# Sums of output-weight blocks on VectorE, in place, and a last token tile in new PSUM banks

## The chip, the cores and the metric

The kernel runs on one core of a Trainium2 chip. The metric is device time in microseconds (us) for one execution. A profiled execution of the kernel also leaves a trace: the start and duration of each instruction on each engine, what ended the idle time in front of it, and the clock that TensorE was granted. Engine names are those of the profile: PE is TensorE (PEld its weight loads), DVE is VectorE, ACT is ScalarE, POOL is GpSimd, SP is SyncE, whose queue issues most DMAs.

## What is computed

One hybrid decoder layer on x (1024 tokens x 1024 features, float32). A first norm and a combined input projection feed two branches, a retention and a gated linear recurrence; both are gated, concatenated to 2048 columns, and pass one output projection, a residual add and a final norm. Cut to what matters here:

```python
h = x
xn = rms_norm(h, norm_in_g)
q, k, v, g_ret, x_lru, g_lru = jnp.split(einsum('btd,de->bte', xn, w_in), IN_SPLITS, axis=-1)
y_ret = group_norm_heads(chunkwise_retention(q, k, v)) * silu(g_ret)   # 1024 columns
y_lru = rg_lru(conv(x_lru)) * silu(g_lru)                              # 1024 columns
h = h + einsum('bte,ed->btd', concatenate([y_ret, y_lru]), w_out)      # w_out: 2048 x 1024
return rms_norm(h, norm_out_g)
```

The change lies in the last part: the retention's half of the output projection, y_ret (1024 x 1024) times the upper half of `w_out` (1024 x 1024), and the norm behind it.

## The kernel before

Every product of two float32 matrices is made from three matmuls in a rounded format: each operand is split by `split` into a high part (a cast on ACT, L106) and a low part (a subtraction on DVE, L107), and `mm3` (L112) issues high x high, high x low and low x high. A block of 256 rows x 512 columns of weights is one tile of 128 partitions x 2 x 512, so a cast or subtraction of it is 128x1024 (called wide below); a piece of 128 tokens x 512 columns is 128x512 (half-wide).

The program runs in stages: input projection, gates and recurrence; then `w_out`'s lower half (the recurrence's share) with the retention's work put in between as `fillers`; then the last stage. Instructions are written in Python order, but a scheduler sets the order on each engine's own queue, and each queue is worked in order: what waits at its head holds all behind it.

The last stage computes four quarter products (two token halves x two column halves) with seven products instead of eight. They run in the order P1, P2, P5, P6, P7, P3, P4; each has four token tiles (t = 0 to 3) of 12 matmuls of 128x512. The weight operands, with Wkc the block of row half k and column half c:

- P1: W11, P2: W21, P3: W22
- P5: W11+W12, P6: W11+W12+W22, P7: W12+W22, P4: W11+W12+W22+W21

`w_load` (L893) makes such a sum while it loads: SP loads the first block into a tile pair, and POOL issues one DMA for each further block that adds it to what lies there (L901, `accum_op`). One accumulating DMA must have landed before the next of the same tile is issued. `w_parts` (L905) then splits both tiles into high and low parts. On the other side `combine` (L188, DVE) makes sums of the retention's output blocks `ys`, which `y_block` (L911) reads back from memory, and `y_parts` (L917) splits them.

PSUM has eight banks here. `A[t]` holds P1, then P6, P7 and P4 on top of it; `E[t]` holds P5 and P3; P2 uses the banks that E takes afterwards. `block_add` (L993 to 996) adds a bank to the result tile `h`. After P7, A and E are both added to the second token half; P3 may only write `E[t]` once that is done. P4 closes `A[t]` for t = 0 to 2; its last tile, t = 3, is made in two halves of 256 columns in the same bank `A[3]`, so that the norm of the first half can start. Then follows the norm of each of the eight token tiles (`square`, `norm_first`, `norm_last`, L956 to 986): a square with its row sum on ACT (L958), a square root on ACT (L975), a few 128x1 operations on DVE, a scaling of one column half on ACT (L982) and of the other on DVE (L984), and two stores.

SBUF on the left holds the retention's tiles (`kn`, `sm`, `gch`, `st`, `yn`, `ot`, pool stack `ret`) to the end of the program, with the final norm's `gain2` and `junk` above them.

Of the kernel before, what the change touches and what calls it, by code (L numbers as in the profile page):

```python
# [11 lines left out]
F32R = mybir.dt.float32r  # L12
I32 = mybir.dt.int32
AF = mybir.ActivationFunctionType
ALU = mybir.AluOpType

P = 128
# [23 lines left out]
def hybrid_layer(  # L41
# [17 lines left out]
    pe, act, dve, pool, sp = nc.tensor, nc.scalar, nc.vector, nc.gpsimd, nc.sync  # L59
# [3 lines left out]
    HALF = D // 2  # L63
# [3 lines left out]
    def pool_on(side, name, bufs):  # L67
        return tc.tile_pool(name=name, bufs=bufs, side=side, reuse_waits="tile")
# [6 lines left out]
    def psum():  # L75
        return ps_p.tile([P, 512], F32, name="pp", tag="pp")
# [622 lines left out]
    for j in range(2):  # L699
# [4 lines left out]
    op = {n: ctx.enter_context(pool_on("right", n, k)) for n, k in (  # L704
        ("wraw", 3), ("y0", 2), ("wo", 10), ("qkc", 4), ("yl", 14), ("vc", 4), ("h", 8))}
# [24 lines left out]
    for t in range(NT):  # L730
        r = op["h"].tile([P, T], F32, name="h", tag="h")
# [8 lines left out]
    yl = {}  # L740
# [12 lines left out]
        fill()  # L753
    ph_stack.close()
    ph_next = {}
    ret = ctx.enter_context(ExitStack())
    mask_sb = gwp.tile([P, H, P], F32, name="mask", tag="gw")
    sp.dma_start(out=mask_sb, in_=mask_in)
    for name, n in (("kn", 2), ("sm", 2), ("gch", 3), ("st", 4),
# [1 line left out]
        ph_next[name] = ret.enter_context(pool_on("left", name, n))  # L761

    ph_next["vc"] = op["vc"]
    fin = ctx.enter_context(pool_on("left", "fin", 1))
    junkp = ctx.enter_context(pool_on("left", "junk", 2))


    def heads(f):
# [117 lines left out]
    wt, ys, xop = {}, {}, {}  # L886

    def block(pl):
        return [op[pl].tile([P, 2, 512], F32, name="blk", tag=pl) for _ in range(2)]

    wr = {}

    def w_load(name, pl, *blocks):  # L893

        r = wr[name] = block(pl)
        for i in range(2):
            for j, (kh, ch) in enumerate(blocks):
                src = w_out[kh * HALF + i * 256:kh * HALF + (i + 1) * 256, ch * HALF:(ch + 1) * HALF] \
                    .rearrange("(k p) c -> p k c", p=P)
                if j:  # L900
                    pool.dma_start(out=r[i], in_=src, accum_op=ALU.add)  # L901
                else:
                    sp.dma_start(out=r[i], in_=src)

    def w_parts(name):  # L905
        r = wr.pop(name)
        wt[name] = Parts(op["yl"], "yl")
        for i in range(2):
            wt[name].put(i, r[i])

    def y_block(f, th):  # L911
        ys[f, th] = block("wo" if f or th else "y0")
# [4 lines left out]
    def y_parts(name, src):  # L917
        pl = "qkc" if name in ("P2", "P6", "P3") else "wo" if name == "P4" else "yl"
        xop[name] = Parts(op[pl], pl)
        for i in range(2):  # L920
            xop[name].put(i, src[i])

    for dh in range(2):
        cols = slice(dh * HALF, (dh + 1) * HALF)
        w_cur = w_o
        for t in range(NT):
            if dh == 0 and 0 < t < NT - 1:
                load_yl(t + 1)
            if dh == 0 and t == 2:
                w_o = group(D, HALF, (0,))  # L930
            ps = psum()
            unit_o(ps, yl[t], w_cur, slice(0, HALF), (3, 7) if dh == 0 else (2, 5, 7))
            r = hres[t][:, cols]
            with tc.issue_after(last_load[0].ins):
                sp.dma_start(out=r, in_=x[t * P:(t + 1) * P, cols])
            dve.tensor_tensor(out=r, in0=ps, in1=r, op=ALU.add)
            if dh == 0 and t == NT - 2:
                w_o += group(D, HALF, (2, 4, 6))
            if dh == 1 and t == 2:
                w_load("P1", "wraw", (0, 0))  # L940
                w_parts("P1")
            if dh == 1 and t == 4:
                w_load("P2", "wraw", (1, 0))
                w_parts("P2")
            if dh == 1 and t == 5:
                y_block(0, 0)
                y_parts("P1", ys[0, 0])
            if dh == 1 and t == 6:
                y_block(1, 0)
                w_load("P5", "wraw", (0, 0), (0, 1))  # L950
    gain2 = fin.tile([P, T], F32, name="gain2")
    sp.dma_start(out=gain2, in_=g_out.partition_broadcast(P))
    dve.tensor_tensor(out=gain2, in0=gain2, in1=gain2, op=ALU.add)
# [34 lines left out]
    def product(name, ps, t, first, last, cols=slice(0, 512)):  # L988
        for k in range(4):
            mm3(ps, xop[name].token(k, t), tuple(a[:, cols] for a in wt[name].row(k)),  # L990
                first and k == 0, last and k == 3)

    def block_add(t, th, ch, ps, op_=ALU.add, cols=slice(0, 512)):  # L993
        r = hres[4 * th + t][:, ch * HALF + cols.start:ch * HALF + cols.stop]
        dve.tensor_tensor(out=r, in0=r, in1=ps, op=op_)  # L995
        return r

    A, E = [psum() for _ in range(4)], []
    for t in range(4):
        product("P1", A[t], t, True, False)  # L1000
        block_add(t, 0, 0, A[t])
        fill()
        if t == 0:
            y_parts("P2", ys[1, 0])
    while fillers:
        fill()
    y_block(0, 1)
    y_block(1, 1)
    w_parts("P5")
    combine(s1 := block("wo"), ys[0, 1], ys[1, 1], ALU.subtract)  # L1010
    y_parts("P5", s1)
    for t in range(4):
        ps = psum()
        product("P2", ps, t, True, True)
        block_add(t, 0, 0, ps)
        norm_first(t, 0)
    w_load("P6", "wraw", (0, 0), (0, 1), (1, 1))
    w_parts("P6")
    combine(s1, s1, ys[0, 0], ALU.subtract)
    y_parts("P6", s1)  # L1020
    for t in range(4):
        E.append(psum())
        product("P5", E[t], t, True, False)
    w_load("P7", "wraw", (0, 1), (1, 1))
    w_parts("P7")
    s3 = ys[0, 1]
    combine(s3, ys[0, 0], s3, ALU.subtract)
    y_parts("P7", s3)
    for t in range(4):
        product("P6", A[t], t, False, False)  # L1030
        block_add(t, 0, 1, A[t], ALU.subtract)
    w_load("P4", "y0", (0, 0), (0, 1), (1, 1), (1, 0))
    w_load("P3", "wraw", (1, 1))
    w_parts("P3")
    s4 = ys[1, 0]
    combine(s4, s1, s4, ALU.add)
    y_parts("P3", s4)
    for t in range(4):
# [1 line left out]
        block_add(t, 1, 1, A[t], ALU.subtract)  # L1040
        block_add(t, 1, 1, E[t])
        norm_first(4 + t, 1)
    y_parts("P4", ys[1, 1])
    w_parts("P4")
    for t in range(4):
        product("P3", E[t], t, False, True)
        r = block_add(t, 0, 1, E[t])
        square(ssum[:, t, 1:2], r)
        norm_last(t, 1, ssum[:, t, 1:2])
    for t in range(4):  # L1050
        mean, part = ssum[:, 4 + t, 0:1], ssum[:, 4 + t, 1:2]
        cuts = [0, 512] if t < 3 else [0, 256, 512]
        for c0, c1_ in zip(cuts, cuts[1:]):
            cols = slice(c0, c1_)
            product("P4", A[t][:, cols], t, False, True, cols)
            square(part, block_add(t, 1, 0, A[t][:, cols], ALU.add, cols))
            if c1_ < 512:
                dve.scalar_tensor_tensor(out=mean, in0=part, scalar=1.0 / D, in1=mean,
                                         op0=ALU.mult, op1=ALU.add)
                part = small.tile([P, 1], F32, name="part", tag="part")  # L1060
        norm_last(4 + t, 0, part)
# [69 lines left out]
```

## Time and profile before

| what | value |
|---|---|
| time, median of 3 runs | 774.28 us (772.71 to 774.65) |
| the profiled execution: time / span of its instructions | 770.49 us / 768.7 us |
| PE busy | 729.0 us, 95% of the span |
| DVE busy | 575.8 us, 75% |
| ACT busy | 426.2 us, 55% |
| POOL busy | 17.4 us, 2%, of which 17.2 us are the 14 accumulating DMAs |
| mean granted PE clock | 0.981 |
| chain that ended last, by engine | PE 59%, ACT 14%, DVE 13%, DMA 7% |

The whole-span shares are averages. The stage of the change starts near 663 us, where P1's first matmul runs, and lasts to the end, so it has to be read by itself: in which stretches PE waits, and what ends each wait.

### The profile page before, as it was taken

To read this page: it belongs to the slowest core of one execution; us is meant where nothing else is said; L and a number is where in the kernel's file an instruction comes from. 1 tells how busy PE (TensorE), PEld (TensorE's weight loads), DVE (VectorE), ACT (ScalarE), POOL (GpSimd) and SP (SyncE) were. 2 spreads that over 40 slices of the span, in tenths; PEclk is the share of its full clock that TensorE was granted. 3 is DMA by queue.
4 is the path that set the end of the run, shared out by engine and by line. 5 is a ranking of instruction groups with operands and counts; after the bars stand their busy time and mean duration, and the time that the engine had idled before them with its cause. 6 is when DMAs were issued, how large, how long until landed. Compare 5 with 4: busy or idle time off the path is not lost.

```text
span 768.7 us, 9387 instructions
## 1 busy us (share of the span) xinstructions
PE 729.0 (95%) x3448; PEld 604.5 (79%) x3448; DVE 575.8 (75%) x950; ACT 426.2 (55%) x649; POOL 17.4 (2%) x18
## 2 busy tenths in 40 slices
PE   6989999999999999999999999997999999999764
PEld 5777888887787888788788888887899998888553
DVE  6998647669977968976899887874675667589355
ACT  6785435695599689679533333335453454244134
POOL 0000000000000000000000000000000011111100
PEclk9999999999999999999999999999999999999987
DMA  8752712140214213422445544599987686687534
GB/s 303 277 192 83 246 54 69 55 133 32 76 48 165 69 55 99 134 83 75 145 125 128 132 111 109 146 284 291 311 274 259 212 263 152 191 185 143 82 83 164
DMA packets 98015, 116.07 MB, mean 151 GB/s; under 512 B 5169, under 2 KB 66737, under 8 KB 97969
## 3 DMA queue, kind: packets, MB, share of 16 engines
q1 hardware_dynamic: 94160, 108.13, 44.5%
q0 software_dynamic: 3808, 7.34, 6.1%
q8 instruction: 27, 0.44, 0.2%
q14 instruction: 20, 0.16, 0.1%
HBM read 86.09 MB, written 29.36 MB: 150 GB/s over the span
## 4 chain that ended last, share of the span: by engine, by line
PE 59%; ACT 14%; DVE 13%; DMA 7%; issue 5%; SPq 1%; POOL 0%; ACTq 0%; DVEq 0%; POOLq 0%
PE pp L112 51%; PE pp L796 2%; PE pp L835 2%; PE pp L834 2%; DMA bt<-in_w_in 1%; DVE xc L561 1%; PE pp L817 1%; DVE wq L107 1%; DVE y L614 1%; PE pp L856 1%; DMA xt<-in_x 1%; ACT wq L106 1%; DMA graw<-in_gate_w 1%; DMA vc<-v_d 1%; ACT L601 1%
## 5 line engine op out<-in xcount | busy, mean ns | idle before, releaser
L112 PE MATMUL pp<-wh,wq 128*128 128x512 f32 x960 | 301.6, 391 | 1.8 <-DVE cy L471 0.9
L112 PEld LDWEIGHTS pp<-wh,wq 128*128 128x128 f32 x960 | 179.9, 188 | 42.8 <-ACT cy L461 2.4
L112 PE MATMUL pp<-wl,wq 128*128 128x512 f32 x480 | 186.9, 389 | 0.0
L112 PEld LDWEIGHTS pp<-wl,wq 128*128 128x128 f32 x480 | 90.1, 188 | 18.6
L112 PE MATMUL pp<-wo,yt 128*128 128x512 f32 x384 | 97.9, 402 | 0.0
L112 PEld LDWEIGHTS pp<-wo,yt 128*128 128x128 f32 x384 | 70.4, 191 | 13.0
L107 DVE TENSOR_TENSOR wq<-t,wq 128x1024 fp32r<-128x1024 f32 x40 | 48.7, 1221 | 38.8 <-ACT wq L106 31.7
L106 ACT CAST wq<-t 128x1024 fp32r<-128x1024 f32 x40 | 41.7, 1051 | 31.6 <-PE pp L112 26.6
L112 PE MATMUL pp<-wh 128*128 128x512 f32 x112 | 45.9, 410 | 8.3 <-ACT wh L106 8.3
L112 PE MATMUL pp<-wh,w 128*128 128x512 f32 x160 | 52.9, 391 | 0.1
L112 PE MATMUL pp<-wl,wh 128*128 128x512 f32 x112 | 45.1, 404 | 0.0
L106 ACT CAST ylh<-blk 128x1024 fp32r<-128x1024 f32 x20 | 20.5, 1049 | 43.2 <-DMA blk<-in_w_out 28.8
L112 PE MATMUL pp<-wh,wl 128*128 128x512 f32 x112 | 43.9, 396 | 0.1
L112 PEld LDWEIGHTS pp<-wh,w 128*128 128x128 f32 x160 | 30.0, 188 | 6.8 <-DVE w L107 0.5
L461 ACT COPY cy<-pp 128x512 f32<-128x512 f32 x20 | 11.6, 580 | 41.8 <-PE pp L112 41.2
L848 ACT ACTIVATE yn<-pp,nb,rs_y 128x128 f32<-128x128 f32 x64 | 24.0, 457 | 17.0 <-DVE nb L846 17.0
L901 POOL DMA_DIRECT2D blk<-in_w_out x14 | 17.2, 1228 | 713.8 <-DVE ot L858 622.6
L107 DVE TENSOR_TENSOR yll<-blk,ylh 128x1024 fp32r<-128x1024 f32 x20 | 24.1, 1221 | 11.3 <-ACT ylh L106 11.2
L112 PEld LDWEIGHTS pp<-wh 128*128 128x128 f32 x112 | 21.9, 195 | 13.5 <-ACT wh L106 8.7
L112 PE MATMUL pp<-ylh,qkch 128*128 128x512 f32 x48 | 20.3, 422 | 12.3 <-DVE h L995 12.3
L112 PE MATMUL pp<-wl,w 128*128 128x512 f32 x80 | 31.1, 389 | 0.0
L422 ACT CAST wq<-wraw 128x512 fp32r<-128x512 f32 x40 | 22.9, 617 | 9.3 <-PE pp L112 8.4
(183 smaller groups left out, 1358.5 us busy)
## 6 DMA issues: line engine op xcount, KB each, us to landing
wraw<-in_w_in SPq DMA_DIRECT2D x40, 512.0 KB, 4.9
qkc<-qk_d SPq DMA_DIRECT2D x16, 512.0 KB, 5.9
blk<-in_w_out SPq DMA_DIRECT2D x14, 512.0 KB, 4.5
blk<-in_w_out POOLq DMA_DIRECT2D x14, 512.0 KB, 5.7
bt<-in_w_in SPq DMA_DIRECT2D x20, 256.0 KB, 5.4
xA<-in_xT SPq DMA_DIRECT2D x16, 256.0 KB, 5.4
v_d<-vo SPq DMA_DIRECT2D x16, 256.0 KB, 2.5
xt<-in_x SPq DMA_DIRECT2D x8, 512.0 KB, 4.4
```

Source lines behind the costliest of these rows:

```text
L106: act.copy(out=hi, in_=src)
L107: dve.tensor_tensor(out=lo, in0=src, in1=hi.bitcast(F32), op=ALU.subtract)
L112: pe.matmul(ps, a, b, start=first and j == 0, stop=last and j == 2, skip_group_check=True)
L422: act.copy(out=h[:, j], in_=b)
L461: act.copy(out=self.cy[:, :TH], in_=self.A)
L561: dve.scalar_tensor_tensor(out=xc[:, d:], in0=c[:, :T - d], scalar=cw[3 - d], in1=xc[:, d:], op0=ALU.mult, op1=ALU.add)
L601: act.activation(out=a, in_=r, func=AF.Exp, scale=c1[:, b:b + 1])
L796: heads(lambda h, hs: pe.matmul(psc[:, hs], k[:, hs], q[:, hs], start=True, stop=True))
L834: pe.matmul(po[:, hs], q[:, hs], st[:, h], start=True, stop=False)
L835: pe.matmul(po[:, hs], sm[:, h], vn[:, hs], start=st is None, stop=True)
L848: heads(lambda h, hs: act.activation(out=yn[:, hs], in_=po[:, hs], func=AF.Identity, scale=rs[:, h:h + 1], bias=nb[:, h:h + 1]))
L901: pool.dma_start(out=r[i], in_=src, accum_op=ALU.add)
```

## The change

It does five things. `w_load` loads one plain block, by SP alone; POOL issues no DMA any more. `w_parts` takes a second block and adds it to the first on DVE, in place, before the split: P5's sum is W11 += W12, P6's adds W22 to that, P4's adds W21, and P7's is W12 += W22; that makes eight wide additions. The retention's space is given back before the stage, and a new pool `lw` of six tiles lies there: the blocks W22 and W21 and the low part of P4's weights (its high part goes to `y0`). P4's split is written between P7's token tiles, not after them. And A[3] is added to `h` by itself during P3, after which P4's last tile starts anew in two fresh PSUM banks, one for each half.

```diff
+    fin = ctx.enter_context(pool_on("left", "fin", 1))
+    junkp = ctx.enter_context(pool_on("left", "junk", 2))
+    ret = ExitStack()
...
-    def w_load(name, pl, *blocks):
-
+    def w_load(name, pl, kh, ch):
         r = wr[name] = block(pl)
         for i in range(2):
-            for j, (kh, ch) in enumerate(blocks):
...
-                if j:
-                    pool.dma_start(out=r[i], in_=src, accum_op=ALU.add)
-                else:
-                    sp.dma_start(out=r[i], in_=src)
...
+    def w_parts(name, src, add=None, dst=None):
+
+        w = wt[name] = object.__new__(Parts)
+        w.hi, w.lo = [[op[pl].tile([P, 2, 512], F32R, name="wt", tag=pl) for _ in range(2)]
+                      for pl in (("y0", "lw") if name == "P4" else ("yl", "yl"))]
         for i in range(2):
-            wt[name].put(i, r[i])
+            r = wr[src][i]
+            if add:
+                o = wr[dst or src][i]
+                dve.tensor_tensor(out=o, in0=r, in1=wr[add][i], op=ALU.add)
+                r = o
+            wt[name].put(i, r)
...
+    while fillers:
+        fill()
+    ret.close()
+    op["lw"] = ctx.enter_context(pool_on("left", "lw", 6))
     A, E = [psum() for _ in range(4)], []
+    w_load("12", "wo", 0, 1)
     for t in range(4):
         product("P1", A[t], t, True, False)
         block_add(t, 0, 0, A[t])
-        fill()
...
-    w_parts("P5")
+    w_load("22", "lw", 1, 1)
+    w_load("21", "lw", 1, 0)
+    w_parts("P5", "11", "12")
...
-    w_load("P6", "wraw", (0, 0), (0, 1), (1, 1))
-    w_parts("P6")
+    w_parts("P6", "11", "22")
...
-    w_load("P7", "wraw", (0, 1), (1, 1))
-    w_parts("P7")
+    w_parts("P7", "12", "22")
...
-    w_load("P4", "y0", (0, 0), (0, 1), (1, 1), (1, 0))
-    w_load("P3", "wraw", (1, 1))
-    w_parts("P3")
+    w_parts("P3", "22")
...
         norm_first(4 + t, 1)
-    y_parts("P4", ys[1, 1])
-    w_parts("P4")
+        if t == 1:
+            w_parts("P4", "11", "21")
+        elif t == 2:
+            y_parts("P4", ys[1, 1])
     for t in range(4):
         product("P3", E[t], t, False, True)
+        if t == 3:
+            block_add(t, 1, 0, A[t])
...
-            product("P4", A[t][:, cols], t, False, True, cols)
-            square(part, block_add(t, 1, 0, A[t][:, cols], ALU.add, cols))
+            ps = A[t][:, cols] if t < 3 else psum()[:, cols]
+            product("P4", ps, t, t == 3, True, cols)
+            square(part, block_add(t, 1, 0, ps, ALU.add, cols))
```

Up to the retention's last token tile the order on every engine is the one before. Three places of the last stage are shown. The first is DVE after product P7. In the kernel before, `yll_6026` is the low part of P4's second weight tile and the `h` rows are the additions of A (pp_5596) and E (pp_5809, pp_5822) that P3 has to wait for:

```order
L995 TENSOR_TENSOR h_3798<-h_3798,pp_5809 128x512 [waits DVE_49]
L107 TENSOR_TENSOR yll_6026<-blk_5912,ylh_6024 128x1024 [waits DMASW5_49,Activation_49]
L964 TENSOR_SCALAR ssum_5592<-ssum_5592 128x1 [waits Activation_49]
L965 TENSOR_TENSOR h_3798<-h_3798,gain2_5589 128x512 [waits DVE_49]
L995 TENSOR_TENSOR h_3799<-h_3799,pp_5596 128x512 [waits PE_49]
L995 TENSOR_TENSOR h_3799<-h_3799,pp_5822 128x512 [waits DVE_49]
```

and now, where L909 is the new addition of W21 and `wt_5978`, `wt_5979` are the low parts of P4's weights:

```order
L997 TENSOR_TENSOR h_3796<-h_3796,pp_5600 128x512 [waits PE_49]
L107 TENSOR_TENSOR wt_5978<-blk_5548,wt_5976 128x1024 [waits DVE_49]
L997 TENSOR_TENSOR h_3796<-h_3796,pp_5798 128x512 [waits DVE_49]
L997 TENSOR_TENSOR h_3797<-h_3797,pp_5601 128x512 [waits PE_49]
L909 TENSOR_TENSOR blk_5549<-blk_5549,blk_5681 128x1024 [waits DMAHW2_49]
L966 TENSOR_SCALAR ssum_5590<-ssum_5590 128x1 [waits Activation_49]
L967 TENSOR_TENSOR h_3796<-h_3796,gain2_5587 128x512 [waits DVE_49]
L997 TENSOR_TENSOR h_3797<-h_3797,pp_5811 128x512 [waits DVE_49]
L107 TENSOR_TENSOR wt_5979<-blk_5549,wt_5977 128x1024 [waits Activation_49]
```

P4's low part still stands between these additions, but what it waited for from the accumulating DMAs (DMASW5) is now an addition on DVE itself of a block that SP loads.

The second place is SP's queue around P1. In the kernel before, `blk<-o_d` are the retention's outputs of the second token half and `blk<-in_w_out` the first blocks for P5's second tile, P6 (two), P4, P3 (two), P4:

```order
L859 DMA o_d_77<-ot_5569 128x4x128 [waits DVE_49]
L903 DMA blk_5758<-in_w_out 128x2x512 [waits DMAHW4_49,DMASW0_49,DVE_49]
L914 DMA blk_5661<-o_d_77 128x2x512 [waits DMAHW5_49,DMAHW3_49,DMAHW6_49,DMAHW0_49,PE_49]
L914 DMA blk_5662<-o_d_77 128x2x512 [waits PE_49]
L903 DMA blk_5835<-in_w_out 128x2x512 [waits DMASW1_49,DVE_49]
L903 DMA blk_5836<-in_w_out 128x2x512 [waits DMASW3_49,DVE_49]
L903 DMA blk_5911<-in_w_out 128x2x512 [waits DMAHW1_49,DVE_49]
```

and now, where blk_5604 and blk_5605 are W12, blk_5676 and blk_5677 W22, and blk_5680 and blk_5681 W21:

```order
L896 DMA blk_5604<-in_w_out 128x2x512 [waits DMAHW0_49,PE_49]
L896 DMA blk_5605<-in_w_out 128x2x512 [waits DMAHW1_49,PE_49]
L916 DMA blk_5668<-o_d_77 128x2x512 [waits DMAHW3_49,DMAHW6_49,DMAHW2_49,PE_49]
L916 DMA blk_5669<-o_d_77 128x2x512 [waits PE_49]
L859 DMA o_d_77<-ot_5567 128x4x128 [waits DMAHW4_49,DVE_49]
L896 DMA blk_5676<-in_w_out 128x2x512 [waits DMAHW5_49,Activation_49]
L896 DMA blk_5677<-in_w_out 128x2x512 [waits Activation_49]
L916 DMA blk_5672<-o_d_77 128x2x512 [waits DMAHW7_49,DMAHW4_49,PE_49]
L916 DMA blk_5673<-o_d_77 128x2x512 [waits DMAHW0_49,PE_49]
L896 DMA blk_5680<-in_w_out 128x2x512 [waits DMAHW1_49]
L896 DMA blk_5681<-in_w_out 128x2x512 [waits DMAHW2_49]
```

All weight loads now stand close together, two of them ahead of the retention's blocks, and behind the last of them come only the stores of the result.

The third place is DVE at the start of the stage. `ot` is the gated output of the retention's last token tile, which SP stores and reads back for P5, and blk_5548, blk_5549 are the two tiles of W11. In the changed kernel there stands:

```order
L909 TENSOR_TENSOR blk_5548<-blk_5548,blk_5604 128x1024 [waits DMAHW0_49]
L858 TENSOR_TENSOR ot_5567<-pp_5562,gch_5299 128x512 [waits DMAHW6_49,DMAHW4_49,PE_49]
L938 TENSOR_TENSOR h_3799<-pp_5552,h_3799 128x512 [waits PE_49]
L107 TENSOR_TENSOR wt_5686<-blk_5548,wt_5684 128x1024 [waits Activation_49]
L909 TENSOR_TENSOR blk_5549<-blk_5549,blk_5605 128x1024 [waits DMAHW7_49,DMAHW1_49]
```

where before stood

```order
L858 TENSOR_TENSOR ot_5569<-pp_5564,gch_5299 128x512 [waits DMAHW7_49,DMAHW5_49,PE_49]
L936 TENSOR_TENSOR h_3799<-pp_5554,h_3799 128x512 [waits PE_49]
L107 TENSOR_TENSOR yll_5667<-blk_5548,ylh_5665 128x1024 [waits DMASW0_49,Activation_49]
L995 TENSOR_TENSOR h_3792<-h_3792,pp_5593 128x512 [waits PE_49]
L995 TENSOR_TENSOR h_3793<-h_3793,pp_5594 128x512 [waits PE_49]
```

The first new addition, which waits for the load of W12, stands ahead of the retention's last `ot`.

## Rows read from the trace of the kernel before

**Rows 1.** Busy time by stretch: PE, PEld, DVE, ACT, POOL, PEclk, DMA, GB/s.

```profile
663.70:718.30 54.60, 54.60 (x241) 44.86 (x239) 39.88 (x47) 20.00 (x26) 8.63 (x8) 1.00 0.71 159
718.30:740.30 22.00, 9.78 (x37) 7.66 (x36) 10.56 (x18) 4.75 (x9) 3.54 (x3) 0.84 0.46 72
```

**Rows 2.** Timeline of PE: start us, us; in brackets idle before and releaser.

```profile
723.67 0.76 PE L112 MATMUL pp<-ylh,qkch 128*128 128x512 f32 x1 [5.37 <-DVE h L995]
724.23 0.63 PE L112 MATMUL pp<-yll,qkch 128*128 128x512 f32 x1
724.66 0.63 PE L112 MATMUL pp<-ylh,qkcl 128*128 128x512 f32 x1
...
740.33 0.79 PE L112 MATMUL pp<-ylh,qkch 128*128 128x512 f32 x1 [6.88 <-DVE h L995]
...
759.23 0.58 PE L112 MATMUL pp<-ylh,woh 128*128 128x256 f32 x1 [4.78 <-DVE h L995]
```

**Rows 3.** Chain that ended last, 663 to 739 us: start us, us, what.

```profile
663.42 53.31 PE pp L112 x235
...
724.23 1.21 POOL blk L901
...
730.24 5.67 DMA blk<-in_w_out
735.99 1.05 ACT ylh L106
737.07 1.22 DVE yll L107
...
738.95 0.61 DVE h L995
```

**Rows 4.** Timeline of DVE and ACT, wide and half-wide operations, 695 to 710 us.

```profile
695.92 3.49 DVE L188 TENSOR_TENSOR blk<-blk 128x1024 f32<-128x1024 f32 x3
...
705.87 1.06 ACT L106 CAST ylh<-blk 128x1024 fp32r<-128x1024 f32 x1 [3.62 <-PE pp L112]
...
707.93 1.22 DVE L107 TENSOR_TENSOR yll<-blk,ylh 128x1024 fp32r<-128x1024 f32 x1
709.07 0.68 DVE L995 TENSOR_TENSOR h<-h,pp 128x512 f32<-128x512 f32 x1
709.66 1.22 DVE L107 TENSOR_TENSOR qkcl<-blk,qkch 128x1024 fp32r<-128x1024 f32 x1
```

**Rows 5.** Timeline of DVE and ACT, one token tile's norm, and the end.

```profile
751.97 0.68 DVE L995 TENSOR_TENSOR h<-h,pp 128x512 f32<-128x512 f32 x1
752.69 0.63 ACT L958 ACTIVATE junk<-h 128x512 f32<-128x512 f32 x1 [0.66 <-DVE h L995]
...
753.44 0.29 ACT L975 ACTIVATE root<-ssum 128x1 f32<-128x1 f32 x1
...
754.42 0.72 ACT L982 ACTIVATE h<-h,half 128x512 f32<-128x512 f32 x1 [0.68 <-DVE half L980]
754.42 0.75 DVE L984 SCALAR_TENSOR_TENSOR h<-h,half,gain 128x512 f32<-128x512 f32 x1
755.09 0.68 DVE L995 TENSOR_TENSOR h<-h,pp 128x512 f32<-128x512 f32 x1
...
762.20 0.42 DVE L995 TENSOR_TENSOR h<-h,pp 128x256 f32<-128x256 f32 x1 [1.31 <-PE pp L112]
...
764.17 0.75 DVE L984 SCALAR_TENSOR_TENSOR h<-h,half,gain 128x512 f32<-128x512 f32 x1
```

**Rows 6.** SP's and DVE's timeline by the loads; landing of the blocks' loads.

```profile
658.93 0.87 SPq L914 DMA_DIRECT2D blk<-o_d  x2
663.46 0.69 DVE L858 TENSOR_TENSOR ot<-pp,gch 128x512 f32<-128x512 f32 x1 [2.02 <-PE pp L856]
664.17 0.36 SPq L859 DMA_DIRECT2D o_d<-ot  x1
666.58 0.87 SPq L914 DMA_DIRECT2D blk<-o_d  x2
671.58 1.23 DVE L188 TENSOR_TENSOR blk<-blk 128x1024 f32<-128x1024 f32 x1 [1.51 <-DMA blk<-o_d]
...
DMA to landing us min/median/max: 3.9/4.9/8.1
```

More of the change, by code (lines that the diff above doesn't have):

```diff
@@ L755, in hybrid_layer @@
     ph_next = {}
-    ret = ctx.enter_context(ExitStack())
+    fin = ctx.enter_context(pool_on("left", "fin", 1))
+    junkp = ctx.enter_context(pool_on("left", "junk", 2))
+    ret = ExitStack()
     mask_sb = gwp.tile([P, H, P], F32, name="mask", tag="gw")
@@ L763, in hybrid_layer @@
     ph_next["vc"] = op["vc"]
-    fin = ctx.enter_context(pool_on("left", "fin", 1))
-    junkp = ctx.enter_context(pool_on("left", "junk", 2))
     def heads(f):
@@ L891, in hybrid_layer @@
     wr = {}
-    def w_load(name, pl, *blocks):
+    def w_load(name, pl, kh, ch):
         r = wr[name] = block(pl)
         for i in range(2):
-            for j, (kh, ch) in enumerate(blocks):
-                src = w_out[kh * HALF + i * 256:kh * HALF + (i + 1) * 256, ch * HALF:(ch + 1) * HALF] \
-                    .rearrange("(k p) c -> p k c", p=P)
-                if j:
-                    pool.dma_start(out=r[i], in_=src, accum_op=ALU.add)
-                else:
-                    sp.dma_start(out=r[i], in_=src)
-    def w_parts(name):
-        r = wr.pop(name)
-        wt[name] = Parts(op["yl"], "yl")
-        for i in range(2):
-            wt[name].put(i, r[i])
+            sp.dma_start(out=r[i], in_=w_out[kh * HALF + i * 256:kh * HALF + (i + 1) * 256,
+                                             ch * HALF:(ch + 1) * HALF]
+                         .rearrange("(k p) c -> p k c", p=P))
+    def w_parts(name, src, add=None, dst=None):
+        w = wt[name] = object.__new__(Parts)
+        w.hi, w.lo = [[op[pl].tile([P, 2, 512], F32R, name="wt", tag=pl) for _ in range(2)]
+                      for pl in (("y0", "lw") if name == "P4" else ("yl", "yl"))]
+        for i in range(2):
+            r = wr[src][i]
[4 more added lines that the diff above has]
+            wt[name].put(i, r)
     def y_block(f, th):
@@ L939, in hybrid_layer @@
             if dh == 1 and t == 2:
-                w_load("P1", "wraw", (0, 0))
-                w_parts("P1")
+                w_load("11", "wraw", 0, 0)
+                w_parts("P1", "11")
             if dh == 1 and t == 4:
-                w_load("P2", "wraw", (1, 0))
-                w_parts("P2")
+                w_load("21", "wraw", 1, 0)
+                w_parts("P2", "21")
             if dh == 1 and t == 5:
@@ L949, in hybrid_layer @@
                 y_block(1, 0)
-                w_load("P5", "wraw", (0, 0), (0, 1))
+                w_load("11", "wraw", 0, 0)
     gain2 = fin.tile([P, T], F32, name="gain2")
@@ L1001, in hybrid_layer @@
         block_add(t, 0, 0, A[t])
-        fill()
         if t == 0:
             y_parts("P2", ys[1, 0])
-    while fillers:
-        fill()
     y_block(0, 1)
     y_block(1, 1)
-    w_parts("P5")
+    w_load("22", "lw", 1, 1)
+    w_load("21", "lw", 1, 0)
+    w_parts("P5", "11", "12")
     combine(s1 := block("wo"), ys[0, 1], ys[1, 1], ALU.subtract)
```

## The prediction, made before the changed kernel was run

> **What bounds the kernel now.** I read the stage of the change by itself, from P1's first matmul near 663.5 us to the end. Busy time by stretch comes first: up to 718.3 PE is busy in every microsecond at a granted clock of 1.00, and from 718.3 to 740.3 for 9.78 of 22.0 us at 0.84 [rows 1]. So the loss begins after P7. PE's timeline shows where: three waits, 5.37 us ahead of P3, 6.88 ahead of P3's last tile and 4.78 ahead of the second half of P4's last tile, each put down to an addition of DVE to h [rows 2]. The chain that ended last then says what DVE itself waited for: POOL's accumulating DMAs, 6.0 us from one issue to the next (724.23, 730.24), the last one's landing, ACT's cast of P4's second tile, its low part on DVE, and only then the additions that free E[3] [rows 3]. The first wait is the same chain for P4's first tile. The third is another thing: both halves of P4's last tile lie in bank A[3], and the second may not be written before DVE has read the first.
>
> After each wait matmuls start slowly: 0.43 us from one 512-wide matmul to the next (724.23, 724.66), the rate of the 1.2 GHz level, against 53.31 / 235 = 0.227 us in the unbroken run [rows 2, 3].
>
> **What goes: PE.** Without the waits P3 and P4 follow P7 at 718.2. P3's 48 and P4's 36 full matmuls take 84 x 0.227 = 19.1 us, the 24 half-wide ones half each, 2.7, together 21.8: PE would end at 740.2 with the last result out. Before, it ended as DVE's last addition began, 762.2 [rows 5]. **PE: -22.0 us** (17.0 of waits, the rest from the lower clock behind them).
>
> **What comes: DVE.** The eight sums are wide additions of two SBUF tiles. L188 does exactly that: three in 3.49 us, the last counted whole at 1.22, so 1.14 from one to the next; a low part takes the same (707.93 to 709.07), a half-wide addition 0.59 to 0.60 (709.07 to 709.66) [rows 4]. Eight cost 9.1 us. DVE has 39.88 of 54.6 us busy up to 718.3, ACT 20.0 [rows 1], so they fit there, but they leave little idle, and the question becomes when DVE is done.
>
> The rows show 73% for DVE in that stretch. The Trainium skill, "Perfetto Trace Analysis", section "Optimizing Scalar/DVE Operations", advises to move work off DVE to another engine when DVE is saturated; the change moves work onto it. What that makes of the time, if the sums lie on the path, is the second rival.
>
> I follow DVE's queue in the order shown. Its first sum waits for W12. That load takes the buffer that the retention's block took before, so it can be issued at 658.93 like that one [rows 6]; landing times of such blocks were 3.9 to 8.1, median 4.9, so it is there at 663.8 and the sum ends at 665.0. Behind it in the queue stands `ot`, which ran at 663.46; it slips by about 1.2 us, and with it SP's store of it, which was issued at 664.17. Behind that store now stand W22's two loads, the reading back of the retention's outputs (666.58 before) and W21's loads. W22's first tile is issued at 665.7 and lands, by the median, at 670.6. There P6's first sum begins; I count from here, since DVE has no larger gap afterwards. Up to the last subtraction of A[3] behind P7 stand 33 wide operations, 24 half-wide ones and 7 small ones: 33 x 1.14 + 24 x 0.60 + 7 x 0.07 = 52.5 us. The sum for P5's left operand may wait for the retention's outputs, which come 1.2 us later than at 671.58 behind 1 MB more of loads: I add 1.2 us (0 to 4). DVE then comes to P3's first addition at 724.3.
>
> Is PE held up meanwhile? P5 starts at 685.5, and its last low part is done near 682; P6 starts at 696.4, its parts near 695; P7 at 707.3, P3 at 718.2, both with several microseconds in hand; E[3] is freed about 725.5, just before P3's last tile at 726.4. ACT waits for a weight buffer until P6's last tile, as it waited 3.62 us for one before P7 [rows 4]; behind that cast stand P3's and P4's, but DVE reaches their low parts only after 707. So I take PE as unbroken, and P3's last tile as the tightest place.
>
> **The closing part.** From a tile's addition to the next one was 755.09 - 751.97 = 3.12 us, in lock step: addition, square on ACT, root, four 128x1 operations, scaling [rows 5]. The new order puts a tile's scaling behind the next tile's addition. A period is then addition and hand-over (to ACT's square, 0.72), the square up to the point where the next ACT operation can start (0.73, an estimate from 752.69 to the root at 753.44 and its hand-over), the other half's scaling on ACT (0.63 to 0.72), root (0.29) and 0.45 for the next two small operations before the next addition: about 2.85. From DVE's arrival at P3's first addition: 3.3 us to the third tile's (A[3]'s addition and one more scaling lie between), four periods, 11.4, to the seventh, 1.25 to the first half of the last tile, 1.95 to the second, and from there to the end of the last scaling as before, 764.92 - 762.20 = 2.7 [rows 5]. Sum 20.6: 744.9. PE has long been done by then (740.2), so of PE's 22.0 us DVE gives back about 2.
>
> **Sum.** The last scaling ended at 764.92 and will end at 744.9: **-20.0 us**. What follows it (stores, end of the program) stays. The profiled execution took 770.49 us, so 750.5; the median of the runs shown is 3.8 us above that execution, and I take the same 20.0 off it: **754.3 us**.
>
> Costed at nothing: the new places of the retention's tiles (queue orders there are unchanged, and the one load of gates that now waits for the last store of q and k stands just ahead of a load that waits for it anyway; without that cover it would cost that store's landing, some 4 us); P4's lost wait on POOL; closing the pool stack (all of the retention's work is queued before P1 already).
>
> The price of the loads hangs on landing. The Trainium skill, "DMA: Bandwidth & Descriptors", section "Anatomy of one DMA", fits 2.0 us plus bytes / 436 GB/s, 3.2 us for 512 KB (an estimate by that page, for DMAs from POOL); with it W22 would land 1.7 us sooner and the time would be 752.6. The rows say 3.9 at the least, so the sum keeps the median.
>
> **Rivals.**
> 1. *DVE later than I count.* For it: one late block at the longest landing shown, 8.1 instead of 4.9, shifts the whole queue by 3.2 us, since it has no gaps left; or the closing part keeps 3.12 us a tile, 8 x 0.27 = 2.2 more. Against it: the median. Time 756.5 to 757.5.
> 2. *The sums lie on the path.* If ACT or a load leaves DVE idle as it was before, the eight sums add their 9.1 us to the end rather than fill gaps: -22.0 + 9.1 = -12.9, 761.4. For it: ACT's wait for a buffer in the middle of the stage. Against it: 14.7 us of DVE's idle time in the first stretch [rows 1].
> 3. *The change does half of what it says.* P4's low part still stands between the additions that P3 needs. If W21's sum comes late there, only the wait inside A[3] goes (4.78, and 1.4 of slow matmuls) and half of the other two with theirs (15.2 / 2): -13.8, 760.5. Against it: W21 is loaded some 40 us ahead of its sum.
> 4. *Slower: PE's clock.* Products that run on through P3 and P4 in ever new banks could fall to the lower level. Price 0.20 us a matmul of 512 (0.43 - 0.227); from 100 slow ones, two products, the gain is gone; if all of P5, P6, P7, P3 and P4 ran so, 228 x 0.20 + 24 x 0.10 = 48 us, 802 us. Against it: 235 matmuls in a row from 663 to 717 at 1.00 [rows 1, 3], in changing banks. The Trainium skill, "TensorE: Matmul & The Clock Gate", section "A second HAM failure mode: psum-queue depth-cycling", tells of a kernel whose clock swung because PE idled briefly while cycling through banks; by this trace the drops stand behind the three long waits alone, and those go.
>
> **How the numbers follow.** Forecast 754.3 (DVE a microsecond or two off): 0.62. Rival 1: 0.20. Rival 2: 0.07. Rival 3: 0.05. Rival 4: 0.02. DVE keeps pace with PE and nothing is given back, -22.0, 752.3, or a little below it by the spread of the runs: 0.04. Range 751.5 to 759.5: it takes in that bound less a run's spread and rival 1 with both its causes and the spread of medians, and leaves out rivals 2 to 4 and odd ends, some 0.18. A measurement here tells about 0.3% (2.3 us) from no change; all cases but rival 4 and something unforeseen lie far below: faster 0.95, same 0.02, slower 0.03.
>
> **What would show it.** PE's timeline has no wait over 1 us after 663 us and ends near 740; the granted clock is 1.00 to there; POOL issues nothing; DVE is over 90% busy from 670 to 723; the chain that ended last runs through DVE and ACT from about 725 on at under 3 us a tile. Wrong would be: a DMA wait of several microseconds on DVE at the first sums (rival 1), DVE idle in mid-stage behind ACT's casts (rival 2), a PE wait ahead of P3 (rival 3), a clock below 1.00 without a wait before it (rival 4).

## The result and the profile after

The changed kernel took **749.13 us** in the median (747.83 to 750.35, 4 runs), the kernel before beside it 773.5 (771.13 to 774.65): ratio 0.9689, 95% interval 0.9658 to 0.9719. The forecast was 754.3, with a range from 751.5 to 759.5: faster, as foretold, by more than the range allowed. The profiled execution took 750.35 us, its span 748.6. Two of the runs of the kernel before (852.64 and 1222.96 us, at a mean granted clock of 0.82 and 0.56) are in no median of this document.

Busy time by stretch in the kernel after (the columns of [rows 1]; the third stretch is the rest):

```profile
663.70:718.30 54.60, 54.60 (x242) 45.18 (x242) 51.42 (x62) 23.04 (x30) 0.00 (x0) 1.00 0.24 81
718.30:740.30 22.00, 21.77 (x108) 18.25 (x106) 20.08 (x55) 13.08 (x36) 0.00 (x0) 1.00 0.34 126
740.30:748.60 8.30, 0.00 (x0) 0.00 (x0) 2.94 (x10) 2.41 (x7) 0.00 (x0) 0.68 0.48 176
```

In the second stretch PE was busy for 9.78 us at a clock of 0.84 [rows 1]; now it is for 21.77 at 1.00. POOL does nothing, and DVE has 51.42 us of 54.6 where it had 39.88. PE's waits of [rows 2] are all gone: after 655 us PE waits for nobody, and its last matmul starts at 739.79.

DVE's timeline at the places that the prediction counted from (columns as in [rows 4]):

```profile
662.88 1.23 DVE L909 TENSOR_TENSOR blk<-blk 128x1024 f32<-128x1024 f32 x1 [1.64 <-DMA blk<-in_w_out]
664.02 0.68 DVE L858 TENSOR_TENSOR ot<-pp,gch 128x512 f32<-128x512 f32 x1
...
670.00 2.36 DVE L909 TENSOR_TENSOR blk<-blk 128x1024 f32<-128x1024 f32 x2
...
675.07 1.23 DVE L188 TENSOR_TENSOR blk<-blk 128x1024 f32<-128x1024 f32 x1 [2.11 <-DMA blk<-o_d]
...
723.88 3.07 DVE L997 TENSOR_TENSOR h<-h,pp 128x512 f32<-128x512 f32 x5
```

L909 is a sum of two weight blocks. The first one pushes `ot` from 663.46 [rows 6] to 664.02, and the sum for P5's left operand waits 2.11 us for the retention's outputs.

The last part of the chain that ended last (start us, us, what), to be read beside [rows 5]:

```profile
730.33 0.61 DVE h L997
730.96 0.73 ACT junk L960 x2
731.68 0.61 ACT h L984
732.30 0.20 ACT root L977
...
732.93 0.61 DVE h L997
...
735.54 0.61 DVE h L997
...
743.37 0.75 DVE h L986
```

From one tile's addition to the next are 2.6 us, where it was 3.12; the scaling of the other half (L984) now lies between square and root. The last scaling ends at 744.12; before, at 764.92. What follows it did not stay as it was. SP's last two stores in the kernel before:

```profile
764.92 0.33 SPq L983 DMA_DIRECT2D out<-h  x1
765.34 0.38 SPq L986 DMA_DIRECT2D out<-h  x1
```

and after:

```profile
744.11 0.33 SPq L985 DMA_DIRECT2D out<-h  x1
744.84 0.33 SPq L988 DMA_DIRECT2D out<-h  x1
```

The last store is issued 0.72 us behind the end of the scaling, where it was 0.42, and from the end of the scaling to the end of the execution are 6.23 us, where it was 5.57. No run shows why.

### The profile page after: what moved, and what is told of

Its sections match the earlier page's. It is cut to its first block, busy times and chain, and to the rows that moved or that the text cites. A ratio compares the mean times of both kernels' runs of the same rounds, so it can differ in the third digit from the quotient of the medians.

```text
span 748.6 us, 9355 instructions
## 1 busy us (share of the span) xinstructions
PE 723.9 (97%) x3448; PEld 601.0 (80%) x3448; DVE 583.5 (78%) x959; ACT 425.1 (57%) x649; POOL 0.2 (0%) x4
## 4 chain that ended last, share of the span: by engine, by line
PE 51%; DVE 21%; ACT 15%; DMA 8%; issue 4%; SPq 0%; DVEq 0%; ACTq 0%
PE pp L112 42%; DVE h L997 2%; DVE xc L561 2%; PE pp L835 2%; PE pp L796 2%; PE pp L834 2%; DVE wt L107 2%; PE pp L817 1%; DVE wq L107 1%; DVE y L614 1%; DMA xt<-in_x 1%; ACT wq L106 1%; PE pp L856 1%; ACT L601 1%; DVE blk L188 1%
## 5 line engine op out<-in xcount | busy, mean ns | idle before, releaser
L106 ACT CAST wq<-t 128x1024 fp32r<-128x1024 f32 x40 | 41.7, 1050 | 31.4 <-PE pp L112 26.6
L112 PE MATMUL pp<-wt,ylh 128*128 128x512 f32 x96 | 29.5, 389 | 0.0
L112 PE MATMUL pp<-wt,qkch 128*128 128x512 f32 x96 | 29.5, 389 | 0.0
L424 DVE TENSOR_TENSOR wq<-wraw,wq 128x512 fp32r<-128x512 f32 x40 | 26.8, 683 | 0.1
L106 ACT CAST wt<-blk 128x1024 fp32r<-128x1024 f32 x14 | 14.6, 1048 | 21.5 <-PE pp L112 17.7
```

The costliest lines, as they stand in the source:

```text
L106: act.copy(out=hi, in_=src)
L112: pe.matmul(ps, a, b, start=first and j == 0, stop=last and j == 2, skip_group_check=True)
L424: dve.tensor_tensor(out=l[:, j], in0=b, in1=h[:, j].bitcast(F32), op=ALU.subtract)
```

## The experiments

Two lengths are used below. The *entry* is the start of `ot` of the last token tile on DVE, the *stage* runs from there to the end of the last scaling: 663.46 and 101.46 us before, 664.02 and 80.10 after. (After, `ot` itself stands behind the first sum. PE's last transpose for it starts at 662.95, and before at 663.14, so the sum delays `ot` by 0.75 us in this trace, and by 0.60 and 0.75 in two more of after. For a comparison with before the stage is 80.7 to 80.9.)

### Both kernels once more

The profiled pair had moved by 20.1 us, as forecast; the medians by 24.4. So the first question was where other executions of before lose more.

> The kernel before, unchanged, once more, for a second trace of it. The profiled execution shown so far (770.49 us) lies below all four timed ones (771.13 to 774.65, median 773.5). Theory A: the 3 us arise where the change works, in POOL's chain of accumulating DMAs. Then a slower execution has P1's start and P7's end where they were (663.5 and 718.2 us), but links of more than 6.0 us or late landings, and the three PE waits behind 718 us sum to more than 17.0 us: about 20 in an execution of 773.5. Theory B: they arise ahead of the stage (a late landing of a load somewhere before 655 us), alike in both kernels. Then P7's end moves by as much as the span does, and the three waits stay at 17.0 within 0.5.

Measured: 771.62 us (12 runs), before beside it 772.16, ratio 1.0002 (0.9982 to 1.0023); the profiled one 771.21. It entered at 661.39, 2.07 us earlier, and ended at 765.65, 0.73 later. PE's timeline in it:

```profile
723.97 0.77 PE L112 MATMUL pp<-ylh,qkch 128*128 128x512 f32 x1 [7.72 <-DVE h L995]
...
741.06 0.79 PE L112 MATMUL pp<-ylh,qkch 128*128 128x512 f32 x1 [6.62 <-DVE h L995]
...
759.96 0.58 PE L112 MATMUL pp<-ylh,woh 128*128 128x256 f32 x1 [4.29 <-DVE h L995]
```

PE came to P3 two microseconds sooner and waited for them there: 18.63 us in three waits against 17.03. The 2 us came from far ahead: a wait of 2.18 us near 43 us for ACT, itself behind a late load of x, was 0.51 here. Theory B explains the entry of this trace, but not where the gain went. POOL's timeline does, first of the kernel before (start us, us, in brackets idle before and releaser):

```profile
670.84 1.21 POOL L901 DMA_DIRECT2D blk<-in_w_out  x1 [16.71 <-DMA blk<-in_w_out]
679.31 1.22 POOL L901 DMA_DIRECT2D blk<-in_w_out  x1 [7.26 <-DMA blk<-in_w_out]
685.24 1.21 POOL L901 DMA_DIRECT2D blk<-in_w_out  x1 [4.71 <-DVE h L995]
691.23 1.22 POOL L901 DMA_DIRECT2D blk<-in_w_out  x1 [4.77 <-DVE qkcl L107]
...
730.24 1.22 POOL L901 DMA_DIRECT2D blk<-in_w_out  x1 [4.80 <-DMA blk<-in_w_out]
```

and of the same kernel in its second trace:

```profile
669.30 1.21 POOL L901 DMA_DIRECT2D blk<-in_w_out  x1 [17.89 <-DMA blk<-in_w_out]
675.61 1.22 POOL L901 DMA_DIRECT2D blk<-in_w_out  x1 [5.10 <-DMA blk<-in_w_out]
683.63 1.21 POOL L901 DMA_DIRECT2D blk<-in_w_out  x1 [6.80 <-DVE h L995]
691.38 1.22 POOL L901 DMA_DIRECT2D blk<-in_w_out  x1 [6.54 <-issue]
...
730.92 1.22 POOL L901 DMA_DIRECT2D blk<-in_w_out  x1 [4.99 <-DMA blk<-in_w_out]
```

Nine steps from the first to the last issue took 59.40 us in the one and 61.62 in the other; two of them 8.02 and 7.75 us where the first trace has 5.93 and 5.99. The step ahead of these two goes the other way, 6.31 against 8.47.

> The kernel after, unchanged, once more. Its profiled execution (750.35 us) was the longest of its four (747.83 to 750.35, median 749.1). Theory A: the chain that varied is gone, so the spread of its executions is smaller than that of the kernel before run beside it (under 2 us against 3.5), and its median stands 20 us below the profiled execution of before but 22.5 to 24 below before's median. Theory B: the spread arises ahead of the stage and is the same for both; medians of more runs come together at a difference of 20 to 21 us, and the 24.4 measured was luck of the draw.

Measured: 747.9 us (743.94 to 750.38, 6 runs), ratio 0.9675 (0.9646 to 0.9705), 24.3 us below before's 772.16. Stage 80.12. Theory A's expected small spread is missing: 6.4 us in six runs. The difference of 20 to 21 that B expected is missing too.

Two more traces of before:

> The kernel before, unchanged, a third trace. Two traces so far: one enters the stage (the retention's last output, ot on DVE) at 663.46 us and needs 101.5 us from there to the end of the last scaling; the other enters at 661.39, without a 2.2 us wait of PE near 43 us, and needs 104.3. Theory A+B: the stage's own length varies by some 3 us with POOL's chain, whatever the entry; so the new trace has links of 6.0 to 6.3 us with one or two of 7 to 8, and 101 to 105 us from entry to end. Theory B alone (the stage is constant, only the entry varies): 101.5 within 0.5.

> The same once more, with the same expectations: theory A+B 101 to 105 us from the stage's entry to the end of the last scaling, theory B alone 101.5 within 0.5. With four traces the mean tells where the profiled execution of before stood: theory A+B puts it at the short end, so that the change is worth 20 us against it and about 23 against the mean.

Measured: 773.25 and 773.28 us. With the two above (us):

| trace of before | wait near 43 us | entry | entry to first of the nine steps | nine steps of POOL | last issue to the end | stage |
|---|---|---|---|---|---|---|
| profiled, shown ahead | 2.18 | 663.46 | 7.38 | 59.40 | 34.68 | 101.46 |
| second | 0.51 | 661.39 | 7.91 | 61.62 | 34.73 | 104.26 |
| third | 1.79 | 664.07 | 7.52 | 61.94 | 34.16 | 103.62 |
| fourth | 0.58 | 663.91 | 7.54 | 61.59 | 34.70 | 103.83 |

What differs lies in POOL's steps; what stands ahead of and behind them agrees within 0.6 us. The execution on which the prediction was made had the shortest chain of four, by 2.2 to 2.5 us. The fourth trace has the short wait near 43 us and enters late all the same, so that wait is not the only thing that sets the entry. Theory A+B holds for before: entry and stage both vary.

> The kernel after, unchanged, beside the next three. Two traces need 80.10 and 80.12 us from the retention's last output (ot on DVE) to the end of the last scaling, while four of before need 101.5, 104.3, 103.6 and 103.8. Expected: 80.1 within 0.3 again, and a median of 748 to 749 us, 23 to 24 us below before's.

Measured: 748.73 us (6 runs), ratio 0.9692 (0.9658 to 0.9727); stage 80.08. Three traces of after, 80.08 to 80.12: without POOL's chain the stage varies by 0.04 us in three traces (by 0.14 us when it is counted from PE's last transpose, 81.03 to 81.17). The entry varies here too. The three traces have the long wait near 43 us (2.46, 2.15 and 2.39) and enter at 663.67 to 664.17; three kernels below that share after's program up to the stage have 0.61 to 0.70 there and enter at 662.43, 661.91 and 661.36.

### The two parts of the change, each alone

```diff
# before, with the new banks alone
+        if t == 3:
+            block_add(t, 1, 0, A[t])
...
-            product("P4", A[t][:, cols], t, False, True, cols)
+            ps = A[t][:, cols] if t < 3 else psum()[:, cols]
+            product("P4", ps, t, t == 3, True, cols)
```

> Before, with only the second part of the change: the last token tile of P4 in new PSUM banks, A[3] added by itself in P3's last round. If PE's third wait (4.78 us and 1.4 of slow matmuls behind it) was worth its length, the time falls by 6.2 us. By the account in the prediction, DVE and ACT close a tile every 3.12 us in lock step there and are late anyway: the second half's addition can come no earlier than some 1.9 us after the first half's (758.76), so about 760.7 instead of 762.20, and the time falls by 1.5 to 2 us, while PE idles less and ends some 5 us earlier.

Measured: 769.39 us (10 runs), ratio 0.997 (0.9947 to 0.9993), some 2.3 us (0.5 to 4.1). Its stage is 102.68 us, with 62.31 us for POOL's nine steps; PE's third wait is gone and the other two (8.15 and 7.27) are not. Taking the nine steps away, 40.4 us are left against 42.1 in the profiled trace of before and 42.6, 41.7 and 42.2 in the others: the banks alone are worth 1.8 us, not the 6.2 of PE's wait with its slow matmuls. A wait of the engine with the most work was worth a third of its price. DVE and ACT were late behind it anyway: in this trace too they close a tile in 3.12 us (additions at 746.77 and 749.89), while PE waits for nobody there.

The other part alone (the diff reversed, applied to after; all else of the change stays):

> After, with the last token tile of P4 back in A[3] (the new banks undone, the sums kept). If the wait inside A[3] costs what it did before (4.78 us and slow matmuls), the time is 6 us above after. By the account in the prediction the last tile's first half is added at about 739 us, the second half's 12 matmuls take 1.4 us and 1 us more until the result is out, and DVE has one wide addition less: its last addition comes within 0.6 us of after's 741.40, so the time is after's within 0.7 us. Of the theories on the spread: A expects a spread as small as after's, B the same for all.

Measured: 748.12 us (747.36 to 748.88, 4 runs), ratio 0.9688 (0.966 to 0.9716). Stage 80.24, against 80.10: the banks are worth 0.1 us once the sums are in. PE's wait in A[3] shrinks from 4.78 [rows 2] to this:

```profile
737.66 0.50 PE L112 MATMUL pp<-wt,woh 128*128 128x256 f32 x2 [0.51 <-DVE h L997]
```

So nearly all of the gain is the other part's, POOL's DMAs gone and the sums on DVE.

### P4's chain left out

```diff
-    w_load("P4", "y0", (0, 0), (0, 1), (1, 1), (1, 0))
+    w_load("P4", "y0", (0, 0))
```

> Before, with P4's weights loaded without accumulation: the six accumulating DMAs of W12, W22 and W21 are left out (P5's, P6's and P7's eight stay, and nothing is added to DVE), so P4 multiplies with W11 alone. If P4's chain is what PE's first two waits come from, both go, with their slow matmuls; the wait inside A[3] shrinks to under 1 us as DVE now follows PE closely, and the time falls to 748 to 751 us, near after's. If the waits belong to DVE's queue or to the earlier links, P3 is still held up and the time stays above 760. By the account of the prediction DVE has 9 us less to do here than in after, and the end lies no more than 1 to 2 us ahead of after's, since PE's end (740) plus 2.7 us is the floor.

This kernel leaves W12, W22 and W21 out of P4. Measured: 753.22 us (749.77 to 755.02, 4 runs), ratio 0.9744 (0.9698 to 0.9789); it entered late (666.67), and its stage is 82.20. The first two waits are gone and the clock stays at 1.00, so P4's six accumulating DMAs were what PE waited for; beside the eight others PE waits for nothing in the stage ahead of P4's last tile. The third wait did not shrink to under 1 us:

```profile
744.41 0.39 PE L112 MATMUL pp<-ylh,woh 128*128 128x256 f32 x1 [2.46 <-DVE h L995]
```

DVE did not follow PE closely, although it had 9 us less to do than after the change. The next run shows why.

### The price of the sums

```diff
             r = wr[src][i]
-            if add:
-                o = wr[dst or src][i]
-                dve.tensor_tensor(out=o, in0=r, in1=wr[add][i], op=ALU.add)
-                r = o
```

> After, with the eight sums left out of DVE: P5, P6, P7 and P4 multiply with the plain blocks, all else stays. It is the price of the sums where they stand. The prediction: DVE gives back 2 us of PE's 22, so without the sums the stage from the last ot to the end of the last scaling falls from 80.1 us to PE's 76.05 plus 2.7, 78.8: the time falls by 1.3 us (0.5 to 2). Rival 2 (the sums lie on the path): it falls by their whole length, 9.1 us. If the sums are hidden whole, it stays.

This kernel leaves the sums out. Measured: 749.67 us (747.05 to 750.46, 4 runs), ratio 0.9704 (0.967 to 0.9739), after's within the spread. `ot` is not pushed back here, so its stage of 80.93 compares with 80.7 to 80.9: nothing is gained. Of the three expectations only the last holds: the sums are hidden whole. But the cover is not what was thought. DVE's timeline without the sums:

```profile
724.22 0.68 DVE L993 TENSOR_TENSOR h<-h,pp 128x512 f32<-128x512 f32 x1
725.69 0.16 DVE L974 SCALAR_TENSOR_TENSOR v<-ssum 128x1 f32<-128x1 f32 x1 [0.79 <-ACT junk L956]
...
726.67 0.75 DVE L982 SCALAR_TENSOR_TENSOR h<-h,half,gain 128x512 f32<-128x512 f32 x1
727.34 0.68 DVE L993 TENSOR_TENSOR h<-h,pp 128x512 f32<-128x512 f32 x1
```

DVE makes P3's first addition at 721.03, 3.5 us sooner than in after, and then closes most tiles in 3.12 us, the lock step of [rows 5], idle while ACT squares. In after the scheduler put these instructions in another order, each tile's scaling behind the next tile's addition, and a tile took 2.6 us. The closing part has two orders, and the lighter DVE got the worse one. The kernel of the run ahead (P4 without its chain) shows the same lock step (additions at 728.56 and 731.68).

The opposite test puts a second wide operation behind each sum:

```diff
                 dve.tensor_tensor(out=o, in0=r, in1=wr[add][i], op=ALU.add)
+                dve.tensor_tensor(out=o, in0=o, in1=o, op=ALU.max)
```

> After, with each of the eight sums followed by a second wide operation on DVE over the same block (the maximum of the block with itself), which changes no value: 9.1 us more on DVE ahead of P3's additions. If DVE stands at its limit in this stage (51.4 of 54.6 us busy), nearly all of it comes through: the stage grows from 80.1 to 88 to 91 us and PE waits some 8 us ahead of P3's last tile. If the stage has as much room as the run without sums suggests (the end did not move when 9.1 us were taken away), it grows by less than 4 us.

Measured: 750.62 us (750.23 to 750.85, 4 runs), ratio 0.9717 (0.9679 to 0.9756), after beside it 748.73. The stage is 82.23: of 9.1 us, 2.1 come through. Busy time by stretch in this run:

```profile
663.00:718.00 55.00, 55.00 (x245) 45.53 (x244) 54.99 (x64) 21.96 (x29) 0.00 (x0) 1.00 0.22 74
718.00:740.00 22.00, 20.71 (x100) 16.67 (x98) 21.98 (x56) 13.59 (x34) 0.00 (x0) 1.00 0.22 80
```

DVE is busy for 76.97 of 77.0 us and PE still waits for only 0.85. The second expectation (under 4 us) held. Little room is left here; a third helping was not tried.

### The order of the closing part

Each tile's small operations and scaling are held back behind the next tile's addition on DVE:

```diff
+    held, added = [], []
+    def late(*args):
+        if held:
+            with tc.issue_after(added[-1].ins):
+                norm_last(*held.pop())
+        if args:
+            held.append(args)
...
-        norm_last(t, 1, ssum[:, t, 1:2])
+        late(t, 1, ssum[:, t, 1:2])
```

> After, with the closing part in a fixed order on DVE: each tile's small operations and scaling stand behind the next tile's addition. Without the sums the end stayed where it was, because the order chosen for the closing part then was addition, square, scaling in lock step, 3.12 us a tile, with DVE idle for 1 us of each; so the end is set by the order of the closing part, not by DVE's load. Theory: with the fixed order a tile takes 2.2 to 2.5 us, DVE catches up with PE by the last tile, and the stage falls from 80.1 to the floor, PE's end at 76.05 plus 2.7, 78.8 (up to 79.5). Rival: ACT's hand-overs keep 2.6 us a tile whatever the order, and the stage stays at 80.1 within 0.3.

Measured: 747.34 us (746.88 to 748.58, 6 runs), ratio 0.9677 (0.9646 to 0.9709); after beside it 748.73, 0.9692 (0.9658 to 0.9727). The intervals overlap, so the times don't tell the two apart. The traces do: stage 79.35 against 80.08 to 80.12. DVE's timeline there:

```profile
732.05 0.69 DVE L1006 TENSOR_TENSOR h<-h,pp 128x512 f32<-128x512 f32 x1 [0.67 <-PE pp L112]
...
734.79 0.69 DVE L1006 TENSOR_TENSOR h<-h,pp 128x512 f32<-128x512 f32 x1 [0.67 <-PE pp L112]
...
737.71 0.40 DVE L1006 TENSOR_TENSOR h<-h,pp 128x256 f32<-128x256 f32 x1
```

Now DVE waits for PE in every tile (2.74 us apart, PE's own pace), and the last addition starts 0.4 us after PE's last matmul (737.31). The theory holds in the one trace that there is: DVE catches up and PE is the floor. The tail behind the last addition is 3.0 us instead of 2.7, so 79.35 and not 78.8.

As a second change on top, P7's and P4's sums on POOL:

```diff
-                dve.tensor_tensor(out=o, in0=r, in1=wr[add][i], op=ALU.add)
+                eng = pool if name in ("P7", "P4") else dve
+                eng.tensor_tensor(out=o, in0=r, in1=wr[add][i], op=ALU.add)
```

> As the one before it, and P7's and P4's four sums made on POOL instead of DVE: 4.6 us less for DVE. Theory (the order of the closing part sets the end): no more than the fixed order alone gives, 78.8 to 79.3 us, since PE's end is the floor. Rival (DVE's lag sets it): 0.5 to 1 us below the run with the fixed order alone. A third case: POOL's sums are several times as slow as DVE's or slow DVE down, and P7 waits for its parts; then the stage is longer than after's 80.1.

Measured: 752.2 us (751.53 to 754.14, 6 runs), ratio 0.9742 (0.9709 to 0.9774); stage 83.40. The third case. POOL's and PE's timelines:

```profile
687.29 2.79 POOL L910 TENSOR_TENSOR blk<-blk 128x1024 f32<-128x1024 f32 x1 [10.61 <-DVE ssum L967]
693.65 3.32 POOL L910 TENSOR_TENSOR blk<-blk 128x1024 f32<-128x1024 f32 x1 [3.56 <-DVE wt L107]
```

```profile
699.85 0.79 PE L112 MATMUL pp<-wt,qkcl 128*128 128x512 f32 x1 [2.42 <-DVE qkcl L107]
```

A sum takes POOL 2.8 to 3.3 us where DVE takes 1.22. PE waits 2.42 us in mid-stage for a low part. DVE's timeline beside these two sums shows how it came to be late:

```profile
688.34 2.84 DVE L910 TENSOR_TENSOR blk<-blk 128x1024 f32<-128x1024 f32 x1
694.69 2.83 DVE L968 TENSOR_TENSOR h<-h,gain 128x512 f32<-128x512 f32 x1
```

The first is a wide sum (1.22 us elsewhere), the second half-wide (0.68). POOL's sums end at 690.08 and 696.97, and these two end 1.10 and 0.55 us later, as if they had begun only then. A third, L188 at 674.69, is long in the same way: two of them take 4.34 us together instead of 2.36. All three read two tiles of SBUF; a DVE addition from PSUM that lies within POOL's first two sums (672.54) takes its usual 0.69. The three lose 5.8 us, more than the 4.6 of sums that left DVE's queue. How much of PE's wait comes from that, and how much from the order that came with it, was not separated.

## Why the prediction was wrong

**What held.** PE's part: it runs on from P1 to P4 at a clock of 1.00 and is done near 740.1 (foretold 740.2). DVE's way: first sum at 662.88 (663.8), P6's first at 670.00 (670.6), P3's first addition near 724.5, the second in a group of five from 723.88 (724.3). The wait for the retention's outputs was 2.11 us instead of 1.2, and `ot` started 0.56 us later than before instead of 1.2; the two errors nearly cancel. The last scaling moved from 764.92 to 744.12, by 20.8 us, against the 20.0 of the sum, mostly because the closing part was sized at 2.85 us a tile and took 2.6. "What follows it (stores, end of the program) stays" was wrong by 0.7 us the other way. So the profiled pair moved by 20.14 us; that the forecast for it, 750.5, comes so near to 750.35 is luck in part.

**The step that failed** is the last of the sum: "the median of the runs shown is 3.8 us above that execution, and I take the same 20.0 off it". It treats the distance between profile and median as something the change leaves alone. In the kernel after the median lies 1.2 us below the profiled execution (749.13 against 750.35). A term taken as +3.8 measured -1.2, and that is 5.0 of the 5.2 us of the miss. Over all runs in this study before has a median of 771.95 us (58 runs) and after 748.63 (16): 23.3 us, not 20.0. The miss divides so:

- 2.3 us: the three runs shown had a median of 774.28, high in the 58. That is luck of the draw, as far as the runs tell.
- 1.5 us: the profiled execution of before lies that far below the median of the 58. The traces put this in POOL's chain, which the change removes: its stage (101.46) was 1.8 us under the mean of the four traces (103.3), its entry 0.2 us later than the mean of theirs.
- 1.2 us: the profiled execution of after lies that far above its median. Its stage is alike in three traces, so this lies ahead of the stage; all three have the long wait near 43 us, and kernels with the short one enter 1.2 to 2.8 us sooner. That the timed runs had the short one more often is likely, but they left no trace that shows it.
- 0.1 us: the profiled pair itself.

The prediction had the row for the second: POOL's links of 6.0 us stood in the chain of waits [rows 3], fourteen DMAs with one landing each behind them, and it priced their removal by the one trace it had. For the loads that stay it did weigh shortest against longest landings; for the DMAs that go, it did not. POOL's DMAs of 512 KB took 5.6 to 8.5 us from issue to landing before, 5.7 in the median. The Trainium skill's page "DMA: Bandwidth & Descriptors", section "Anatomy of one DMA", gives a fit for DMAs from GpSimd that makes 3.2 us of 512 KB (an estimate by that page). The traces disagree: none of these fourteen, which accumulate and run beside other loads, came under 5.6.

**The right sum for a partly wrong reason.** "DVE gives back about 2" came out as 1.3 (744.12 is 4.05 behind PE's end, of which 2.7 is tail). The prediction put it down to DVE's queue filled by the sums. Without the sums the end does not move, and with twice as many it moves by 2.1. More than half of the 1.3 hangs on the order of the closing part, as the run with a fixed order shows by taking 0.75 of it away.

**The rivals.** 1 (DVE later): no; the stage of after is alike in three traces. 2 (sums on the path): no, by the run without them; moving four of them to POOL made the kernel slower. The Trainium skill's "Perfetto Trace Analysis", section "Optimizing Scalar/DVE Operations", says that moving some work off a saturated DVE may make sense, but that between DVE and GpSimd it might not help, since the two share an SBUF read port. The traces agree with the second half: on POOL four sums made the stage 4 us longer, while on DVE all eight, 9.1 us, cost nothing. 3 (half the effect): no PE wait is left. 4 (clock): 1.00 throughout. That nothing is given back (752.3) lies nearest in time, but not in cause: 1.3 us were given back.

What stays open: what makes the first three of POOL's nine steps take 20.4 us together in one execution and 21.2 to 22.1 in the others, what sets PE's wait near 43 us, and why the last store is later.

## What to carry to other kernels

A trace is one draw: a gain that is read off one pair of profiled executions can lie some us from that of the medians, and the distance between a profile and its median is no constant that a change carries along. Before a chain of dependent DMAs is removed, its length should be priced by its slow links too. A wait of the busiest engine is worth what the next engine in line leaves of it (a third, for PE's wait in A[3]), and a lighter engine need not end sooner when the order of its work is chosen anew with it; two experiments, the added work taken away and doubled, show at once how much of it is hidden.

## What was not expected of the hardware

- A chain of accumulating DMAs of 512 KB from POOL took 5.9 to 6.4 us a step in 24 of 36 steps (nine in each of four traces), and 6.6 to 9.5 in the others: 59.4 to 61.9 us for the same nine steps.
- In the second trace of before PE came to the stage 2.07 us sooner, and the kernel still ended 0.73 us later (765.65 against 764.92): a chain 2.2 us longer took it back.
- POOL adds two blocks of 128x1024 in 2.8 to 3.3 us, DVE in 1.22. Meanwhile three DVE operations on two SBUF tiles ended only after POOL's sum, 1.6 to 2.2 us late.
